# The same instructions in another order: an RWKV-7 and gMLP layer whose engine queues are filled by a scheduler that asks a different model of the machine

## The chip, the cores and the metric

The program runs on one core of one Trainium2 chip. A core has five engines with a queue each: TensorE (PE, with its weight loads shown apart as PEld), VectorE (DVE), ScalarE (ACT), GpSimd (POOL) and SyncE (SP). Each works through its queue strictly in the order in which the program was built, and waits on semaphores for the others and for DMA transfers. The metric is the device time of one execution in microseconds. Less is better.

## The reference, cut to what matters

One layer (DEPTH is 1) of a decoder trunk with 1024 channels, for 512 prompt tokens and 8 x 4 sample tokens, 544 columns in all:

```python
proj = xn @ w_in                      # [r | k | v | u | v_g | gate_A | gate_B]
rkv = rkv + (rkv_prev - rkv) * mu_rkv # token shift
decay = exp(-exp(w_log)); a = sigmoid(a0 + (xa @ a1) @ a2); g = sigmoid(xg @ g1) @ g2
def step(S, inp):                     # 16 heads of 64, one token after the other
    sa = einsum('bhij,bhj->bhi', S, -kk_t)
    S = S * w_t + sa * (kk_t * a_t) + v_t * k_t
    return S, einsum('bhij,bhj->bhi', S, r_t)
y = head_norm(y) + sum(rf * kf * r_k) * vf ; o_a = y * g
o_b = gelu(u) * chunk_mix(layernorm(gelu(v_g)))
mixed = sigmoid(ga) * o_a + sigmoid(gb) * o_b ; h = h + rmsnorm(mixed @ w_out)
h = h + rmsnorm(relu(rmsnorm(h) @ w_up)**2 @ w_down)
h = h + sigmoid(h @ w_pg) * (p @ w_pe)
```

Results and inputs are float32.

## The kernel before, in words

**Dense products.** Channels lie on the partitions, tokens on the free axis, in two halves of 288 and 256 columns. A weight block is fetched by SP (L201), rounded to a short form `w_hi` by ScalarE (L191), and the remainder `w_lo` is formed by VectorE (L192). `dense` (L209, its matmul is L214) then issues three matmuls for each 128 rows of weights: `w_hi` by `xh`, `w_hi` by `xl`, `w_lo` by `xh`. Most of TensorE's instructions are these; the text calls them dense matmuls. They do not depend on the recurrence, so they are what TensorE can do while the recurrence waits.

**Time mixing** goes by 8 pairs of heads, and its steps for a pair p are generators:

- `front(p)` (L395) makes r, k, v, the decay and the products of keys inside chunks (matmul L486, VectorE's mask L488 writes `M`), and stores part of `M` to DRAM through POOL's queue (`scr`, L504).
- `solve(p)` (L606) inverts small triangular blocks: POOL fetches them (`Xi`, L612), 28 short VectorE instructions in sequence (L619 and L621) invert them, POOL stores and fetches again (`solved`, L623, then `XD`, L627), VectorE transposes (`XN`, L632), and four rounds of small matmuls (L637, L645, L658, L667) finish the matrix `TT` that the chain needs.
- `chain(p)` (L677) carries the state over 8 chunks. Each chunk is a loop of matmul L687, ScalarE copy L691, matmul L701, ScalarE and VectorE L702 and L703, matmul L706, VectorE L717 (which writes `ZV` for the next chunk's L687). L689 and L707 add to the output and hang beside the loop.
- `samples(p)` (L552) does the sample tokens (L567, L593, L601 among others).
- `back(p)` (L727) normalises the output per head: sums over heads (L349, L350), rows to ScalarE (L358), POOL spreads them over partitions (`st`, L361), VectorE takes an inverse square root (L267 to L274, L364, L365), POOL brings it back (`invy`, L369), TensorE spreads it (L377), and elementwise steps (L740 to L752) with the gate's matmuls L748 to L751 follow.
- `gates(q)` (L755) holds 96 dense matmuls a pair and the elementwise steps L773 to L779; `mixed_in` (L786) turns the result into the operand `hh` or `mx` of the product with w_out (L792, L793).

**What sets the order.** `weave` (L813) interleaves the generators by planned shares (`SPAN`, `GATES`) and so gives each instruction its place in program order; that place is its priority. The Tile framework then keeps, for each engine, a list of instructions whose operands it thinks ready, by a model of how long everything takes, and emits the one of highest priority among them. Every engine's queue is thus fixed when the program is built. The product with w_out, the feed-forward product up, down and the last gate follow after the 8 pairs; they are dense matmuls with their weights streamed. The call that opens the framework's context is L1370 in `kernel`.

## Time and profile before

| | |
|---|---|
| time, median of two runs | 1194.06 us (1193.26 and 1194.86) |
| profiled execution, its own time | 1195.11 us |
| span of the profile | 1193.3 us |
| TensorE busy, weight loads busy | 1159.7 us (97%), 1086.1 us (91%) |
| VectorE, ScalarE, GpSimd busy | 815.6 us (68%), 579.7 us (49%), 108.0 us (9%) |
| granted TensorE clock, mean | 0.999 |
| first chunk of the chain of pair 0, last L706 of pair 7 | 220.5 us, 658.05 us |

The time of the profiled execution lies 1.8 us above its span. Busy time of TensorE is from modelled ends of pipelined matmuls, which overlap each other in the rows: the distance from start to start is what a matmul takes of the queue, not the duration in its row. An `x2` behind a row of the trace says that two instructions are merged in it.

### The profile page before, as it was taken

The numbers are of one execution on the slowest core, as the hardware profiler recorded it, in microseconds if no ns is written. First come the engines' busy times: TensorE is split into PE (matmuls) and PEld (weight loads), VectorE is DVE, ScalarE is ACT, GpSimd is POOL, SyncE is SP. The second block draws the span as 40 slices with busy tenths as digits, with TensorE's granted clock in tenths as the row PEclk, the third lists the DMA queues.
The fourth block names the chain that finished last, engine by engine and source line by source line (L and its number), as shares of the span: only waits on it lengthen the run. The fifth ranks groups of instructions, "written<-read, shape, count | busy, mean of one in ns | idle before, by whom it ended". The sixth has DMA issues, their size and how long they took to land.

```text
span 1193.3 us, 26307 instructions
## 1 busy us (share of the span) xinstructions
PE 1159.7 (97%) x10262; PEld 1086.1 (91%) x10262; DVE 815.6 (68%) x2251; ACT 579.7 (49%) x1406; POOL 108.0 (9%) x199
## 2 busy tenths in 40 slices
PE   7999998999899999999999999999999999999998
PEld 7999997888788888888878998999999999999998
DVE  6795778687878888887876646844563464465584
ACT  6646336557474747464655546642232232233352
POOL 0000012202230221122110000000000000000000
PEclk9999999999999999999999999999999999999999
DMA  6243253211222123141331452222222222222322
GB/s 203 72 126 114 100 159 114 86 50 46 63 74 83 48 64 99 34 118 44 112 95 55 131 171 72 91 81 89 88 89 89 89 89 89 89 89 89 116 73 83
DMA packets 68236, 109.33 MB, mean 92 GB/s; under 512 B 13712, under 2 KB 19760, under 8 KB 68112
## 3 DMA queue, kind: packets, MB, share of 16 engines
q1 hardware_dynamic: 60224, 103.94, 27.6%
q0 software_dynamic: 7600, 3.50, 1.8%
q8 instruction: 81, 1.33, 0.5%
q14 instruction: 43, 0.35, 0.1%
q10 hardware_dynamic: 288, 0.21, 0.1%
HBM read 94.40 MB, written 13.00 MB: 90 GB/s over the span
## 4 chain that ended last, share of the span: by engine, by line
PE 72%; DVE 12%; DMA 7%; ACT 6%; issue 2%; SPq 1%; POOL 0%; DVEq 0%; ACTq 0%; POOLq 0%
PE ps_d L214 47%; PE ps_s L214 3%; PE ps_s L486 2%; PE ps_b L214 2%; PE ps_m L214 2%; DVE w_lo L192 2%; ACT w_hi L191 2%; PE ps_cx L687 1%; PE ps_cx L701 1%; PE ps_cx L706 1%; DMA w_raw<-in_wout 1%; DMA w_raw<-in_wpg 1%; PE ps_cy L707 1%; DVE KR L456 1%; PE ps_m L601 1%
## 5 line engine op out<-in xcount | busy, mean ns | idle before, releaser
L192 DVE TENSOR_TENSOR w_lo<-w_raw,w_hi 128x512 fp32r<-128x512 f32 (+1 forms) x288 | 195.5, 681 | 174.0 <-ACT w_hi L191 169.9
L191 ACT CAST w_hi<-w_raw 128x512 fp32r<-128x512 f32 (+1 forms) x288 | 176.2, 613 | 275.9 <-PE ps_d L214 190.1
L214 PE MATMUL ps_d<-xh,w_hi 128*128 128x256 f32 (+3 forms) x832 | 249.4, 300 | 3.5 <-ACT w_hi L191 2.5
L214 PE MATMUL ps_d<-xl,w_hi 128*128 128x256 f32 (+3 forms) x832 | 246.9, 297 | 0.0
L214 PE MATMUL ps_d<-xh,w_lo 128*128 128x256 f32 (+3 forms) x832 | 246.9, 297 | 0.0
L214 PE MATMUL ps_d<-hh,w_hi 128*128 128x288 f32 (+1 forms) x1200 | 227.7, 288 | 0.0
L214 PEld LDWEIGHTS ps_d<-hh,w_hi 128*128 128x128 f32 x1200 | 188.8, 188 | 0.0
L214 PE MATMUL ps_d<-hh,w_lo 128*128 128x288 f32 (+1 forms) x600 | 173.6, 289 | 0.0
L214 PEld LDWEIGHTS ps_d<-xh,w_hi 128*128 128x128 f32 x832 | 157.5, 189 | 7.5 <-ACT w_hi L191 2.9
L214 PEld LDWEIGHTS ps_d<-xl,w_hi 128*128 128x128 f32 x832 | 157.6, 189 | 4.0 <-issue 3.2
L214 PEld LDWEIGHTS ps_d<-xh,w_lo 128*128 128x128 f32 x832 | 157.1, 189 | 2.2 <-issue 0.8
L214 PE MATMUL ps_d<-ax,w_hi 128*128 128x288 f32 (+1 forms) x704 | 133.3, 288 | 0.0
L214 PEld LDWEIGHTS ps_d<-hh,w_lo 128*128 128x128 f32 x600 | 112.8, 188 | 0.2 <-DVE w_lo L192 0.2
L214 PEld LDWEIGHTS ps_d<-ax,w_hi 128*128 128x128 f32 x704 | 110.3, 188 | 0.4 <-issue 0.2
L214 PE MATMUL ps_d<-ax,w_lo 128*128 128x288 f32 (+1 forms) x352 | 101.5, 288 | 0.0
L214 PEld LDWEIGHTS ps_d<-ax,w_lo 128*128 128x128 f32 x352 | 66.2, 188 | 0.0
L1256 ACT ACTIVATE ax<-t 128x288 fp32r<-128x288 f32 (+1 forms) x64 | 27.5, 430 | 45.4 <-DVE t L1255 45.2
L214 PE MATMUL ps_d<-gx,w_hi 128*128 128x288 f32 (+1 forms) x192 | 41.4, 309 | 6.8 <-ACT gx L853 6.0
L697 ACT ACTIVATE ZP<-ZV,Fp 64x64 f32<-64x64 f32 x96 | 33.1, 345 | 20.7 <-DVE ZV L717 17.3
L214 PEld LDWEIGHTS ps_d<-gx,w_hi 128*128 128x128 f32 x192 | 32.3, 199 | 8.1 <-ACT gx L853 6.0
L1257 DVE TENSOR_TENSOR t<-t 128x288 f32<-128x288 f32 (+1 forms) x64 | 28.1, 439 | 15.7 <-ACT ax L1256 15.3
L361 POOL DMA_DIRECT2D st<-rows x32 | 16.2, 511 | 243.9 <-ACT rows L358 176.8
(455 smaller groups left out, 2295.4 us busy)
## 6 DMA issues: line engine op xcount, KB each, us to landing
w_raw<-in_win SPq DMA_DIRECT2D x112, 256.0 KB, 2.8
w_raw<-in_wup SPq DMA_DIRECT2D x64, 256.0 KB, 2.7
w_raw<-in_wdn SPq DMA_DIRECT2D x64, 256.0 KB, 2.8
w_raw<-in_wout SPq DMA_DIRECT2D x16, 256.0 KB, 3.1
w_raw<-in_wpg SPq DMA_DIRECT2D x16, 256.0 KB, 2.9
w_raw<-in_lora SPq DMA_DIRECT2D x10, 256.0 KB, 2.8
xt<-in_xt SPq DMA_DIRECT2D x8, 276.0 KB, 5.4
ud<-u SPq DMA_DIRECT2D x8, 272.0 KB, 2.2
```

The costliest lines, as they stand in the source:

```text
L191: act.copy(out=hi, in_=raw)
L192: dve.tensor_tensor(out=lo, in0=raw, in1=hi, op=ALU.subtract)
L214: pe.matmul(out, lhsT=w[wi][k - k0], rhs=x[xi][k][:, cols[0]:cols[1]], start=start and n == 0 and j == 0, stop=stop and n == len(ks) - 1 a ...
L361: gp.dma_start(out=st[32 * h:32 * h + 32], in_=rows[h:h + 1].rearrange("o (a b) -> o a b", b=17))
L456: dve.tensor_tensor(out=KR[r, :, 0, h], in0=c3(kk)[r], in1=E[r, :, 0:64], op=ALU.mult)
L486: pe.matmul(p_[:, 256 * ci:256 * ci + 256], lhsT=BK[:, c + ci].rearrange("p a t -> p (a t)"), rhs=KR[:, c + ci].rearrange("p a h t -> p (a ...
L601: pe.matmul(p_[r], lhsT=s["BKTs"][r], rhs=SX[r], start=True, stop=True)
L687: pe.matmul(px[:, 0:128], lhsT=flat(M[:, c, 0]), rhs=flat(ZV[:, c]), start=True, stop=True)
L697: act.activation(out=ZP[r], in_=zv[h][r], func=AF.Copy, scale=F[r, c + 1, 0:1])
L701: pe.matmul(px[:, 0:128], lhsT=TT[:, c], rhs=Xc, start=True, stop=True)
L1256: act.activation(out=hi, in_=t, func=AF.Square)
L1257: dve.tensor_tensor(out=t, in0=t, in1=t, op=ALU.mult)
```

## The change

One argument is added where the framework's context is opened:

```diff
-    with tile.TileContext(nc) as tc:
+    with tile.TileContext(nc, schedule_with_timeline_sim=True) as tc:
         _program(tc, a, o)
```

With it the scheduler's readiness times come from its other model of the machine. The priorities are the same, and so are the instructions, except that ScalarE gets two more activation table loads (at L437 and L1004), because functions from different tables now alternate once more. The order on every engine differs. Three places are shown. Names carry a number, which tells instances of a tile apart.

TensorE, from the L687 of chunk 1 of the chain of pair 6 (`ps_cx_8774`, `ZV_7445`). `SV`, `SX` and `BKTs` belong to the samples, `xh` and `xl` to dense matmuls of `gates`. Before:

```order
L687 MATMUL ps_cx_8774<-ZV_7445,M_7226 128x128
L689 MATMUL ps_cy_8581<-KR_1632,ZV_7445 128x128
L593 MATMUL ps_m_8856<-Ms_7248,SV_7446 64x32 x2
L214 MATMUL ps_d_8951<-xh_93,w_hi_8888 128x256
L701 MATMUL ps_cx_8782<-Xc_8777,TT_2132 128x128
L214 MATMUL ps_d_8951<-xl_101,w_hi_8888 128x256
L214 MATMUL ps_d_8951<-xh_93,w_lo_8889 128x256
L601 MATMUL ps_m_8946<-SX_8947,BKTs_7271 64x512
L706 MATMUL ps_cx_8786<-ZV_7445,BKT_7258 128x128
L707 MATMUL ps_cy_8581<-M_7226,ZV_7445 128x128
```

With the change:

```order
L687 MATMUL ps_cx_8774<-ZV_7445,M_7226 128x128
L689 MATMUL ps_cy_8581<-KR_1632,ZV_7445 128x128
L701 MATMUL ps_cx_8782<-Xc_8777,TT_2132 128x128
L706 MATMUL ps_cx_8786<-ZV_7445,BKT_7258 128x128
L707 MATMUL ps_cy_8581<-M_7226,ZV_7445 128x128
L687 MATMUL ps_cx_8791<-ZV_7445,M_7226 128x128
```

The dense and sample matmuls that stood between the steps of the chain stand earlier now. From the L687 of chunk 1 to that of chunk 7 of this pair there are 87 dense matmuls before and none after; for pair 7 there are 70 and 15.

TensorE, behind the head sums (L349, L350 with `selw`) of the last pair, whose normalisation ends time mixing. `mx` and `hh` are operands of the product with w_out, `invy` is the head inverse that these sums lead to. Before, with 113 dense matmuls between the L350 and the first L377:

```order
L349 MATMUL ps_b_9554<-hs_hi_9550,selw_85 2x256
L350 MATMUL ps_b_9554<-hs_lo_9551,selw_85 2x256
L214 MATMUL ps_d_9696<-xl_107,w_hi_9639 128x256
...
L214 MATMUL ps_d_9962<-mx_9733,w_lo_9971 128x288
L377 MATMUL ps_b_9722<-invy_118,selt_83 128x288
L214 MATMUL ps_d_9963<-mx_9730,w_hi_9970 128x256 x2
```

With the change, with 29 between them:

```order
L349 MATMUL ps_b_9554<-hs_hi_9550,selw_85 2x256
L350 MATMUL ps_b_9554<-hs_lo_9551,selw_85 2x256
L214 MATMUL ps_s_9966<-hh_9908,w_lo_10133 128x288
...
L214 MATMUL ps_m_9967<-hh_9920,w_lo_10133 128x256
L377 MATMUL ps_b_9722<-invy_118,selt_83 128x288
L377 MATMUL ps_b_9724<-invy_118,selt_83 128x256
L748 MATMUL ps_b_9757<-GH0_114,l2hi_9752 128x288
```

What moved out from behind L350 are the dense matmuls of the last gates and most of the product with w_out; they stand ahead of it now.

POOL, the end of its queue: the solve of pair 7 (`Xi_8638`, `solved1_154`, `XD_8941`) and the head inverses of the pairs 5, 6 and 7 (`st` and `invy`). Before:

```order
L504 DMA scr_8238<-M_8211 32x8x32 x4
L612 DMA Xi_8638<-scr_8238 32x16x16 x2
L361 DMA st_8556<-rows_8539 32x1x17 x2
L369 DMA invy_118<-q_8574 1x32x17 x4
L623 DMA solved1_154<-Xi_8638 32x16x16 x2
L627 DMA XD_8941<-solved1_154 32x8x32 x4
L361 DMA st_9138<-rows_9121 32x1x17 x2
```

With the change:

```order
L504 DMA scr_8238<-M_8211 32x8x32 x4
L612 DMA Xi_8638<-scr_8238 32x16x16 x2
L361 DMA st_8556<-rows_8539 32x1x17 x2
L623 DMA solved1_154<-Xi_8638 32x16x16 x2
L369 DMA invy_118<-q_8574 1x32x17 x4
L627 DMA XD_8941<-solved1_154 32x8x32 x4
L361 DMA st_9138<-rows_9121 32x1x17 x2
```

The store of the solved blocks stands ahead of the head inverse of pair 5 now, behind it before. In the feed-forward half TensorE's instructions move by 24 places at most.

## Rows read from the trace of the kernel before

**Rows 1.** The page: span, and engines' busy time, share and instructions.

```profile
span 1193.3 us, 26307 instructions
PE 1159.7 (97%) x10262; PEld 1086.1 (91%) x10262; DVE 815.6 (68%) x2251; ACT 579.7 (49%) x1406; POOL 108.0 (9%) x199
```

**Rows 2.** Stretches: length; busy PE, PEld, DVE, ACT, POOL; clock, DMA share, GB/s.

```profile
200.00:570.00 370.00, 357.80 (x3701) 311.18 (x3699) 303.01 (x1002) 217.03 (x611) 76.53 (x138) 1.00 0.24 67
760.00:1193.00 433.00, 428.19 (x3409) 426.57 (x3407) 234.94 (x506) 143.71 (x292) 0.00 (x0) 1.00 0.29 90
```

**Rows 3.** Chain of waits, 20 to 26 us: start, duration, what.

```profile
22.11 1.59 PE ps_b L214 x12
23.71 1.41 PE ps_cx L214 x12
```

**Rows 4.** PE's timeline, 250 to 255 us, the chain's rows: start, duration, what.

```profile
250.97 0.46 PE L687 MATMUL ps_cx<-ZV,M 128*128 128x128 f32 x2
...
251.79 0.49 PE L701 MATMUL ps_cx<-Xc,TT 128*128 128x128 f32 x2
...
252.84 0.49 PE L706 MATMUL ps_cx<-ZV,BKT 128*128 128x128 f32 x2
...
254.11 0.46 PE L687 MATMUL ps_cx<-ZV,M 128*128 128x128 f32 x2
```

**Rows 5.** Chain of waits, 603 to 624 us: start, duration, what.

```profile
605.30 0.22 PE ps_cy L707 x2
605.52 1.00 PE ps_m L601 x2
```

**Rows 6.** PE's timeline, 568 to 691 us.

```profile
568.68 1.46 PE L486 MATMUL ps_s<-KR,BK 128*128 128x256 f32 x6
...
620.77 0.70 PE L637 MATMUL ps_m<-XN,M 16*32 16x32 f32 x60
...
658.05 0.42 PE L706 MATMUL ps_cx<-ZV,BKT 128*128 128x128 f32 x2
...
665.55 0.28 PE L350 MATMUL ps_b<-hs_lo,selw 128*2 128x256 f32 x1
...
679.93 0.29 PE L377 MATMUL ps_b<-invy,selt 128*128 128x288 f32 x1
...
690.26 0.42 PE L214 MATMUL ps_d<-hh,w_hi 128*128 128x288 f32 x2
```

**Rows 7.** POOL's timeline, 570 to 680 us, DMA issues: start, duration, what [idle before].

```profile
577.54 1.44 POOL L612 DMA_DIRECT2D Xi<-scr  x2 [3.74 <-DMA scr<-M]
...
603.51 1.35 POOL L623 DMA_DIRECT2D solved<-Xi  x2
607.26 2.31 POOL L627 DMA_DIRECT2D XD<-solved  x4 [2.41 <-PE ps_d L214]
...
673.59 1.96 POOL L369 DMA_DIRECT2D invy<-q  x4 [5.75 <-PE ps_d L214]
```

**Rows 8.** VectorE's timeline, 582 to 687 us.

```profile
582.97 0.17 DVE L619 TENSOR_TENSOR tmpi<-Xi 64x14 f32<-64x14 f32 x1 [1.48 <-DMA Xi<-scr]
...
602.04 0.18 DVE L621 TENSOR_TENSOR Xi<-Xi,tmpi 64x14 f32<-64x14 f32 x1
...
620.03 0.44 DVE L632 STREAM_TRANSPOSE XN<-XD 128x256 f32<-128x256 f32 x1
...
683.42 0.72 DVE L742 TENSOR_TENSOR Y<-Y,sv 128x544 f32<-128x544 f32 x1 [0.91 <-ACT Y L741]
...
686.91 0.41 DVE L752 TENSOR_TENSOR Y<-Y,ps_b 128x256 f32<-128x256 f32 x1
```

**Rows 9.** DMA issues, 664 to 680 us: count, KB each, us to landing.

```profile
invy<-q POOLq DMA_DIRECT2D x4, 2.1 KB, 1.6
```

**Rows 10.** A stretch, columns as in the second group.

```profile
623.00:628.00 5.00, 4.52 (x60) 3.81 (x60) 1.43 (x6) 2.95 (x8) 0.00 (x0) 0.66 0.37 111
```

**Rows 11.** Groups by line, ScalarE: count | busy us, mean ns | idle before.

```profile
L1004 ACT ACT_TABLE_LOAD x4 | 5.1, 1283 | 0.1
```

## The prediction, written before the changed kernel ran

> **What bounds the kernel now.** I read the page first: TensorE is busy for 1159.7 of 1193.3 us, no other engine for more than 68% [rows 1]. Whatever the change does, it does by adding to or taking from the time that TensorE's queue spends waiting. Then the stretches: in the feed-forward half weight loads are busy for 426.57 of 433.00 us, so matmuls stand back to back; in the middle, where the pairs run, for 311.18 of 370.00 us [rows 2]. All that can be won or lost lies in time mixing. Third, prices. Twelve dense matmuls of 288 columns take 1.59 us and twelve of 256 columns 1.41 us in the chain of waits, 133 and 118 ns each [rows 3]; a chain or float32 matmul of 128 columns takes 0.22 us, a sample matmul L601 0.50 us [rows 5]. With these I priced the stretches of TensorE's queue between two landmarks in either order ("row cost" below): a stretch cannot be shorter than its row cost, nor than the path of waits through the other engines between the same landmarks. Where the row cost was above the path, the recurrence was hidden; where it falls below, the difference is lost.
>
> **The paths.** One chunk of the chain takes 0.82 us from L687 to L701, 1.05 on to L706 and 1.27 on to the next L687, 3.14 us where nothing else is late [rows 4]. The solve of pair 7 begins behind the last mask matmul L486, which starts at about 569.8 us (the last of six in 1.46 us), and ends at L637, 620.77 us [rows 6]. On it lie: 7.7 us until `Xi` is issued at 577.54 [rows 7], 5.4 until the first of the 28 inversion steps at 582.97, 19.2 until the last ends at 602.22 [rows 8], 3.9 until `XD` is issued [rows 7] with the store's 1.35 and its landing, 4.7 for the issue and as long a landing again (2.4), and 0.7 from `XN` at 620.03 to L637 [rows 8, 6]. The head inverse goes from L350 at 665.55 [rows 6] to the end of the last `invy` issue, 675.55 [rows 7], and the landing of 1.6 us [rows 9]: 11.6 us.
>
> **The change, part by part.** The instructions are the same but for two table loads, and only their order is in question. I walked the two orders of TensorE, POOL and VectorE from landmark to landmark.
>
> *A, the solve of pair 7.* From the last L486 to L637 there are 165 dense matmuls and 44.5 us of row cost before, against 51.0 us real: 6.5 us lost. With the change there are 21 dense matmuls and 17.6 us. The path then rules. The 28 steps last 0.20 us from one to the next (0.40 from L619 to L619) [rows 8], 5.7 us if VectorE does nothing else between, and 12.4 us if it does all of the 16 others that its new order puts there. So the path is 28 to 35 us; I take 33, near the upper end because a queue is strict and the others stand in it. Lost: 33 - 17.6 = 15.4 us, **+8.9** on before (bounds +4 to +11). That POOL now stores the solved blocks ahead of the head inverse of pair 5 saves up to the 1.96 us of four `invy` issues [rows 7], if that inverse would otherwise be ready first; it moves them in front of `XD` instead, so I give it nothing.
>
> *B, the chain of pair 7.* From L637 to the last L706: real 37.3 us [rows 6], row cost 30.8 us before (101 dense matmuls), 6.5 lost. Now 63 dense matmuls, 26.5 us. Of these only 15 stand between the L687 of chunk 1 and that of chunk 7, with 13.8 us of row cost against 6 x 3.14 + 1.87 = 20.7 us of path up to the last L706: 6.9 us lost. The rounds L645 to L667 lie closer too; I add 4 us for them and for small losses, less than the 6.5 of before. **+4.4** (0 to +9). The chain of pair 6, with no dense matmul between its steps, costs nothing of its own, since it runs while the solve of A is waited for; if A were short, it would be 10 us.
>
> *C, the end of time mixing.* From the last L706 to the first product on the last `hh`: real 32.2 us [rows 6], row cost 30.7 before (230 dense matmuls): 1.5 lost. Inside, 113 dense matmuls, 14.2 us, cover the head inverse of 11.6 us. Now 29 of them, 3.6 us, stand there: 8.0 lost. From L377 to the last `hh` matmul it is 10.3 us before [rows 6], of which 2.8 pass between the end of L742 (684.14) and the second L752 (686.91) in waiting for matmuls that stood late [rows 8]; the path is about 7.6. Row cost there falls from 9.9 to 4.0 us: 3.6 lost. **+10.1** (+7 to +12).
>
> The dense matmuls missing in A to C are done earlier, among pairs 0 to 5, at the same price each. Where did TensorE need them there? Its chains have groups of about 24 between steps (3.0 us), close to the whole 3.14 us of a chunk, where before there was 0.5 to 1 us at each step. By row cost against the path their latency loses 10.5 us now and 9.1 before, and the samples of pair 1 stand with gaps of 0.2 to 0.4 us. **+2** for all of it (-8 to +8).
>
> *The clock.* TensorE's granted clock is full except once: 0.66 over 623 to 628 us [rows 10], right behind the small matmuls of the solve, with dense matmuls around. That is one part at 1.2 GHz, the rest at 2.4. The cost is 5 x 0.34 = 1.7 us. After A and C TensorE will have stood idle more than there; two such stretches cost 3.4. **+3** (0 to +8). The Trainium skill says, on the page "TensorE: Matmul & The Clock Gate", section "HAM oscillation — how this bites in real kernels", that a kernel whose matmul bursts are shorter than the waits between them is set back to the low clock at each; by that rule the bursts of A and C would be slow throughout, which is the third rival. The one drop in the trace fits it, and no wait of such length is there to test it.
>
> *The rest.* Two more table loads on ScalarE take 1.28 us each [rows 11]; it is busy 49% [rows 1], and copies of the chain wait behind them at worst: 0 (to +2.6). The same skill's page "ScalarE: Activation LUTs", section "What ACT_TABLE_LOAD costs", adds a drain and gives 2.66 us a load, 5.3 us for both at worst; the rows show 0.1 us of idle before the loads and do not show a drain. In the feed-forward half the order moves by 24 matmuls at most, under 3.2 us of queue; SP's fetches keep their order, so 0.
>
> Sum: 8.9 + 4.4 + 10.1 + 2 + 3 = 28.4 us. The profiled execution took 1195.1 us, 1.0 above the median of the runs, so 1195.1 + 28.4 - 1.0 = 1222.5; I write **1222**.
>
> **Rivals.** *First, not slower:* the large dense groups win time in pairs 0 to 5. In 200 to 570 us weight loads are idle for 58.8 us of 370, where the feed-forward rate would leave 5.6 [rows 2]: about 53 us, 9 for each pair, lost in waits at the steps. If groups of 24 halve that, by letting ScalarE and VectorE answer while TensorE has 3 us to do, 27 us come back and the time is 1222 - 27 = 1195. It decides from 0.8 us a pair on: then the 4.5 us between 1222 and the bound of "slower" are gone. For it speaks that 3.0 us cover each single step of 0.8 to 1.3 us; against it that a group longer than the step delays the chain, and that by the path formula the pairs lose 1.4 us more. Chance 0.2. *Second, nothing changes:* waits only change places, because the row costs by which A to C lose are made up where the shifted matmuls no longer wait; 1195 +- 8. That asks for 28 us of other losses to vanish by chance: 0.05. *Third, the clock:* in A and C and in the chains of pairs 6 and 7 TensorE runs at 1.2 GHz. The 2.8 and 3.6 us of dense matmuls there cost double, the 4.0 too, and some 42 links grow by 0.2 us, the 0.22 us of a chain matmul [rows 5] once more: 10 + 8 = 18 us, 1240. One drop behind small matmuls speaks for it; the full clock in sample stretches against. 0.13. *Fourth, solves of the earlier pairs:* row costs from L486 to L637 of pairs 2 to 6 are 33 to 37 us now, 45 to 62 before, and the path is 28 to 42 us (with the 19.2 us of inversion steps as seen). If they lose 3 us each, 15 us more: 1237. Chance 0.12.
>
> **How the numbers follow.** The forecast has 0.5, with its own range of 1210 to 1236 (half-widths of A 3.5, B 4.5, C 2.5, the early part 8 and the clock 4 added as squares, and a little more). The range of 1199 to 1244 takes it in whole, most of the third and fourth rival, and half of the first. About 2%, 24 us, can be told from no change in this kernel: under 1170 is faster, above 1218 slower. Slower: two thirds of the forecast and nearly all of the third and fourth, 0.33 + 0.24, with a little more for a shape I did not see: 0.60. Same: the rest of the forecast, the first and second, 0.36. Faster needs 52 us from pairs 0 to 5, all that is lost there: 0.04.
>
> **What will show it.** Right: from 570 us on, TensorE is idle for about 15 us between the last L486 and L637, then 1 us in each chunk of the chain of pair 7, 8 us ahead of the last L377 and 3 to 4 behind it; feed-forward as long as before; pairs 0 to 5 within 8 us. Wrong: weight loads clearly denser between 200 and 570 us (first rival), a clock of 0.5 for more than 7 us in all (third), gaps of over 2 us ahead of L637 in pairs 2 to 6 (fourth). If no gap stands ahead of the last L377, the price of dense matmuls was not the measure of that cover.

## The result, and the profile after

The changed kernel takes **1307.13 us** (two runs, 1301.90 and 1312.36) against 1194.06: a ratio of 1.095, with a 95% interval of 1.076 to 1.114. The forecast was 1222 us, within 1199 to 1244. The direction was right, the size was not: 113 us instead of 28. The profiled execution is the longer of the two runs, 1312.36 us, with a span of 1310.6.

The page of the changed kernel: span, TensorE's busy time, and its busy share and granted clock in 40 slices, in tenths.

```profile
span 1310.6 us, 26366 instructions
PE 1212.9 (93%) x10262; PEld 1137.6 (87%) x10262; DVE 823.2 (63%) x2251; ACT 581.8 (44%) x1408; POOL 108.2 (8%) x199
PE   7999999989999898988997887899999999999988
PEclk9899999987988796988997877999999999999999
```

The span is 117.3 us longer than in [rows 1]. TensorE's rows are busy for 53.2 us more with the same instructions, and the time in which it is not busy rises from 33.6 to 97.7 us, 64.1 more. The first part comes with the clock: its mean is 0.934 where it was 0.999, so some 173 us of the span (2 x 0.066 x 1310.6) ran at 1.2 GHz, where it was about 3 (2 x 0.34 x 5 in [rows 10]). The slices with a low digit all lie ahead of the feed-forward half.

Where in the program? The stretches between four landmarks (first L486 of pair 0, last L486 of pair 7, last chain matmul L706, and the product with w_out), columns as in [rows 2]; first before, then after.

```profile
0.00:143.00 143.00, 135.96 (x1019) 130.62 (x1020) 104.28 (x267) 85.35 (x174) 4.94 (x13) 1.00 0.39 124
143.00:570.00 427.00, 411.51 (x4095) 361.88 (x4095) 348.30 (x1126) 244.49 (x669) 86.92 (x156) 1.00 0.27 77
570.00:658.00 88.00, 85.60 (x985) 71.58 (x985) 63.37 (x203) 49.53 (x143) 13.21 (x24) 0.98 0.30 89
658.00:690.00 32.00, 31.01 (x241) 29.93 (x240) 21.89 (x49) 16.12 (x33) 2.96 (x6) 1.00 0.51 149
```

```profile
0.00:163.00 163.00, 145.81 (x1083) 140.79 (x1084) 109.20 (x280) 91.92 (x182) 4.92 (x13) 0.98 0.36 116
163.00:687.00 524.00, 483.49 (x4628) 434.82 (x4627) 371.48 (x1162) 261.83 (x705) 87.07 (x156) 0.90 0.26 74
687.00:775.00 88.00, 71.41 (x553) 55.84 (x552) 47.81 (x165) 38.87 (x116) 13.29 (x24) 0.75 0.15 41
775.00:810.00 35.00, 26.02 (x164) 23.80 (x164) 15.99 (x40) 12.48 (x27) 2.96 (x6) 0.80 0.40 128
```

The last L486 of pair 7 stands at 687 instead of 570 us: all 117 us of delay are there already. From there to the end it takes 623.6 us after and 623.5 before. But the third and fourth stretch hold 432 and 77 rows of matmuls fewer: matmuls of some 46 us of row cost (26.9 in A, 4.3 in B, 14.6 in C, by the counts and prices of the prediction; three quarters of it are dense matmuls) have moved ahead of the landmark. So the end of time mixing lost 46 us more than before, and what lies ahead of it lost 117 - 46 = 71 us more. For the first the prediction had 23.4, for the second 2.

What such a loss looks like: three stretches around the end of pair 3, columns as above, and TensorE's timeline in the middle one.

```profile
478.00:495.00 17.00, 15.54 (x184) 15.26 (x183) 14.34 (x60) 11.39 (x32) 9.63 (x18) 1.00 0.32 86
495.00:519.00 24.00, 19.75 (x214) 16.11 (x213) 15.77 (x42) 9.98 (x28) 0.00 (x0) 0.50 0.06 18
519.00:546.00 27.00, 25.46 (x177) 21.47 (x178) 16.77 (x52) 11.56 (x33) 3.64 (x6) 1.00 0.34 97
```

```profile
499.50 0.76 PE L687 MATMUL ps_cx<-ZV,M 128*128 128x128 f32 x2
500.06 0.63 PE L689 MATMUL ps_cy<-KR,ZV 128*128 128x128 f32 x2
500.62 1.06 PE L658 MATMUL ps_m<-XN,M 32*32 32x32 f32 x32
501.62 0.61 PE L748 MATMUL ps_b<-GH,l2hi 128*128 128x288 f32 x1
...
502.75 0.63 PE L701 MATMUL ps_cx<-Xc,TT 128*128 128x128 f32 x2
503.03 0.80 PE L377 MATMUL ps_s<-invk,selt 128*128 128x288 f32 x2
503.76 1.06 PE L667 MATMUL ps_m<-TT,M 32*32 32x32 f32 x32
507.77 0.58 PE L748 MATMUL ps_b<-GH,l2hi 128*128 128x256 f32 x1 [2.95 <-DVE Y L752]
...
508.79 0.63 PE L706 MATMUL ps_cx<-ZV,BKT 128*128 128x128 f32 x2
509.21 0.63 PE L707 MATMUL ps_cy<-M,ZV 128*128 128x128 f32 x2
```

From 494.5 to 519.4 us there is no dense matmul. Two things are to be seen. L701 to L706 takes 6.0 us where [rows 4] has 1.05: L706 stands behind an L748 of another pair, and that one waits for VectorE, which is 2.95 of the 6.0 us. And the clock is 0.50 throughout: from L706 to L707 it is 0.42 us, where [rows 5] has 0.22 for such a matmul. The stretches on either side, with dense matmuls, ran at 1.00.

### The profile page after: what moved, and what is told of

Its sections match the earlier page's. It is cut to its first block, busy times and chain, and to the rows that moved or that the text cites. A ratio compares the mean times of both kernels' runs of the same rounds, so it can differ in the third digit from the quotient of the medians.

```text
span 1310.6 us, 26366 instructions
## 1 busy us (share of the span) xinstructions
PE 1212.9 (93%) x10262; PEld 1137.6 (87%) x10262; DVE 823.2 (63%) x2251; ACT 581.8 (44%) x1408; POOL 108.2 (8%) x199
## 5 line engine op out<-in xcount | busy, mean ns | idle before, releaser
L191 ACT CAST w_hi<-w_raw 128x512 fp32r<-128x512 f32 (+1 forms) x288 | 176.2, 614 | 263.0 <-PE ps_d L214 167.2
L214 PE MATMUL ps_d<-hh,w_hi 128*128 128x288 f32 (+1 forms) x1200 | 231.6, 290 | 2.9 <-DVE hh L1323 1.2
L214 PEld LDWEIGHTS ps_d<-xh,w_hi 128*128 128x128 f32 x832 | 160.2, 193 | 12.4 <-ACT u L1004 2.1
L214 PEld LDWEIGHTS ps_d<-xl,w_hi 128*128 128x128 f32 x832 | 160.8, 193 | 1.3
L214 PEld LDWEIGHTS ps_d<-xh,w_lo 128*128 128x128 f32 x832 | 160.2, 193 | 1.3 <-issue 0.2
L687 PE MATMUL ps_cx<-ZV,M 128*128 128x128 f32 x128 | 32.5, 341 | 16.4 <-DVE ZV L717 13.4
L486 PE MATMUL ps_s<-KR,BK 128*128 128x256 f32 x128 | 42.9, 482 | 4.1 <-DVE BK L462 4.1
L706 PE MATMUL ps_cx<-ZV,BKT 128*128 128x128 f32 x128 | 33.3, 348 | 12.4 <-DVE ZV L703 12.2
```

The source lines that it names most:

```text
L191: act.copy(out=hi, in_=raw)
L214: pe.matmul(out, lhsT=w[wi][k - k0], rhs=x[xi][k][:, cols[0]:cols[1]], start=start and n == 0 and j == 0, stop=stop and n == len(ks) - 1 a ...
L486: pe.matmul(p_[:, 256 * ci:256 * ci + 256], lhsT=BK[:, c + ci].rearrange("p a t -> p (a t)"), rhs=KR[:, c + ci].rearrange("p a h t -> p (a ...
L687: pe.matmul(px[:, 0:128], lhsT=flat(M[:, c, 0]), rhs=flat(ZV[:, c]), start=True, stop=True)
L706: pe.matmul(pz[:, 0:128], lhsT=s["BKT"][:, c], rhs=flat(ZV[:, c]), start=True, stop=True)
```

## The experiments

In all of them the instructions are those of the kernel, and only the queues differ, unless the text says so. "Held" orders are built by edges that fix the place in an engine's queue and add no wait; the wanted order is taken from a build of either kernel. An engine that is left free is scheduled anew around the held ones. The code is shown shortened.

**Which engine's order?** First TensorE's queue alone as changed, then TensorE's alone as before.

```diff
     with tile.TileContext(nc, schedule_with_timeline_sim=False) as tc:
         _program(tc, a, o)
+        q = _scout(arrays, True)[PE]            # TensorE's queue of the changed kernel
+        for x, y in zip(q, q[1:]): _behind(tc, ins[y], x)
```

> The scheduler of before, but TensorE's queue is forced into the order that the changed kernel has; the four other engines are scheduled around it by the model of before. Theory A (TensorE's order is the cause: the dense matmuls run ahead of the chain, so that the last third of each pair's chain links stands bare): 1270 to 1320 us, with 120 us or more at 1.2 GHz. Theory B (the order on VectorE, ScalarE, POOL and SP is the cause, by steps of the recurrence that stand behind other work there): under 1225 us.

Measured 1330.39 us (ratio 1.111, 1.100 to 1.123), mean clock 0.936, 171 us at 1.2 GHz. Theory A's side, 10 us above its range.

```diff
-    schedule_with_timeline_sim=False ... q = _scout(arrays, True)[PE]
+    schedule_with_timeline_sim=True  ... q = _scout(arrays, False)[PE]
```

> The scheduler of the change, but TensorE's queue is forced into the order that it has before; the other engines are scheduled around it by the changed model. Theory A: 1190 to 1220 us and at most 10 us at 1.2 GHz. Theory B: over 1270 us.

Measured 1306.60 us (1.091, 1.081 to 1.102), mean clock 0.968. Theory B's figure, so neither theory stands alone. Nor do the two runs set TensorE's order against that of the others, because the free engines follow the held one. Counted in the queues as built, VectorE's instructions stand 22.8 places on average from where they stood before in the former run and 2.5 from where they stand in the changed kernel; in this run it is 4.4 and 23.0. For ScalarE it is 16.2 and 0.9, then 1.3 and 16.1. So the former run is nearly the changed kernel on every engine, and TensorE's new order among the others' old ones was not run. This run is nearly the kernel before, with small moves on the other engines, and those alone cost some 110 us. TensorE's longest waits in this run, and then what the kernel before has for the same lines:

```profile
PE ps_s L486 <- DVE BK L462: 13.2, 5, 4.8
PE ps_cx L706 <- DVE ZV L703: 10.1, 12, 1.6
PE ps_cx L701 <- ACT Xc L691: 7.2, 13, 1.6
PE ps_cx L687 <- DVE ZV L717: 6.0, 10, 1.6
```

```profile
PE ps_s L486 <- DVE BK L471: 3.2, 3, 2.7
PE ps_cx L706 <- DVE ZV L703: 1.8, 5, 0.5
PE ps_cx L687 <- DVE ZV L717: 1.3, 6, 0.2
```

The figures are us in total, how often, and the longest. Before, L486's wait for L462 and L701's for L691 are not among TensorE's nineteen longest; L471 also writes `BK`. The matmuls are where they were; what they wait for comes later from VectorE and ScalarE.

**How much does each add?** The old order is held on one engine after the other.

```diff
-    for e in (PE,):
+    for e in (PE, DVE):            # then (PE, DVE, Activation)
```

> The changed scheduler with the queues of TensorE and VectorE forced into the order of before; ScalarE, POOL and SP are scheduled around them by the changed model. With TensorE's queue alone it was 1307 us. If VectorE's order holds what was left of the cost: 1195 to 1230 us. If it lies with ScalarE or the two engines that issue the transfers: 1270 us or more.

Measured 1244.08 us (1.042, 1.036 to 1.049).

> As the former with ScalarE's queue forced too, so that only POOL and SP are left to the changed model. If the three compute engines hold all of the cost: 1192 to 1215 us. If the order in which POOL and SP issue transfers costs much by itself: 1240 us or more.

Measured 1200.75 us (1.0056, 1.0029 to 1.0084). So with TensorE's order as before, holding VectorE's as well wins 63 us, then ScalarE's 43, and POOL and SP are left with 8. These are steps in this sequence; in another the shares could differ. ScalarE surprised me: in the run with TensorE and VectorE held (1244 us), nine in ten of its instructions, casts and others alike, stand within two places of where they stood, and these moves cost 43 us.

**What moved on them?** A weight cast waits until TensorE gives a weight buffer back: on the page of the kernel before, ScalarE is idle for 275.9 us ahead of its 288 casts (L191), 190.1 of them until a dense matmul ended. So casts alone were held.

```diff
+    for e in (DVE, Activation):    # e10: PE and DVE held whole, this for Activation alone
+        for n in before[e]:
+            if n in cast: _behind(tc, ins[n], last)
+            else: last = n
```

> The changed scheduler with TensorE's queue in the order of before (1307 us so far), and with each weight cast (w_hi on ScalarE, w_lo on VectorE) held behind the other instruction that it follows on its engine before; all else is free. Theory D (the model lets casts pass steps of the recurrence; a cast then waits for TensorE to give a weight buffer back, and what stands behind it waits too): 1215 to 1250 us. Theory E (it is the order of the other rows among themselves): 1285 us or more.

Measured 1288.11 us (1.079, 1.066 to 1.091): 18 of some 110 us came back by the medians, and the intervals of the two runs overlap. Theory E's figure.

> As the run with the queues of TensorE and VectorE in the order of before (1244 us), with the casts on ScalarE held as in the former. Theory D: 1200 to 1218 us, since ScalarE's whole queue forced gave 1201. Theory E: 1235 us or more.

Measured 1226.39 us (1.027, 1.018 to 1.036): between the two, 18 of the 43 us.

> All five queues forced into the order of before, but on ScalarE the instructions other than weight casts stand in the order that the changed model gives them around TensorE and VectorE of before; the casts keep their places (each with as many others ahead of it as before). Theory D: 1192 to 1206 us. Theory E: 1225 to 1245 us.

Measured 1221.89 us (1.023, 1.013 to 1.034), 29 us above the kernel before. Theory D explains under half of ScalarE's part; the rest comes from the other rows. They may be copies of the solve or of the products of keys that now stand ahead of a copy of the chain; no run singles them out. In this run TensorE waits 6.7 us for the copy L691 at L701, and 9 of the 22 us by which the chain ends later are lost ahead of the first chunk. Moving the casts alone was not tried.

**Dense matmuls and chain links.** The chain links are the 192 matmuls L687, L701 and L706 of the eight chains. Of the 191 gaps between them 22 hold no dense matmul before, and 99 after. By pairs 0 to 7 these bare gaps are 3, 3, 2, 2, 4, 4, 1, 3 before and 10, 12, 12, 12, 9, 2, 21, 21 after; in the pairs 0, 2, 3 and 4 seven to nine of them follow one another towards the end. So dense matmuls were held back: none further ahead of the links than before.

```diff
+    for n in before[PE]:
+        if n in link: last = n
+        elif n in dense and last and link[last] >= 0:   # e4: >= 6, e12: <= 5 (pair)
+            _behind(tc, ins[n], last)
```

> The changed kernel with one constraint: no dense matmul may stand further ahead of the 192 chain links than it does before; all the rest is left to the changed scheduler. Theory A in its narrow form (it is the dense matmuls alone that ran ahead): 1195 to 1230 us. If the small matmuls' order or the other engines matter as much: 1250 us or more.

Measured 1293.37 us (1.080, 1.070 to 1.091), mean clock 0.963. The narrow form of theory A fails: with the cover back in place (20 bare gaps in the queue as built), the rest of the new order costs some 100 us.

> The same constraint for the links of the pairs 6 and 7 alone, that is for the end of time mixing, where the prediction had put its sum of 23 us. By the changed kernel's trace the end (675 to 825 us) loses some 45 us more than before and the pairs 0 to 5 and what lies ahead of them some 60: theory A gives 1255 to 1280 us. If the loss of the end is what the prediction said: about 1285. If what is won at the end is lost again because the dense matmuls that move back leave the earlier pairs no fuller: within 10 us of the changed kernel, 1300.

Measured 1302.05 us (1.088, 1.077 to 1.098), 5 us below the changed kernel and not to be told from it. The last L706 comes 26 us earlier (748.9 against 775.2), and the rest then takes 17 us longer, because 164 dense matmuls that were moved back stand there. In the queue as built, pair 5 now has 18 bare gaps where the changed kernel has 2: the bareness has moved to another pair.

> The changed scheduler, with dense matmuls held back to where they stand before among the chain links of the pairs 0 to 5 alone; the links of the pairs 6 and 7 stand as bare as the change leaves them (one group of 131 and then mostly none). Against the run that holds them everywhere (1293 us) only the end of time mixing differs, for which the prediction summed 8.9 + 4.4 + 10.1 = 23 us. If that sum is right: 1310 to 1325 us. If the end costs what its stretch in the changed kernel's trace lost on top of before, 45 us: 1330 to 1345. If what the end lacks is covered by something else: 1285 to 1300.

Measured 1291.28 us (1.083, 1.081 to 1.085): 2 us below the run that holds them everywhere. The queue as built is not what I had expected of it: the dense matmuls held back from the pairs 0 to 5 stand ahead of pair 6 and in it, which has 8 bare gaps instead of 21, and 197 of them stand between the last L486 and L637 of pair 7, where the run that holds them everywhere has 129 and the changed kernel 21. As bare as in the changed kernel are the chain of pair 7 (21 gaps) and what follows the last L706. From the last L486 to the last L706 it takes 106.1 us against 87.5, 18.6 more; 6.1 of these are won ahead of that stretch and 14.9 behind it. So the bareness of the prediction's B and C costs nothing here, in a kernel in which the others' orders cost some 100 us already. That of A was not run by itself.

**The clock.** In the changed kernel, all five queues held, four unused matmuls were set behind each of the 101 links with fewer than two dense matmuls behind them: of 256 columns, then of 8.

```diff
+    if (p, c, stage) in _BARE:
+        for _ in range(4):
+            pe.matmul(px[:, 256:256 + 2 * w] ..., lhsT=blk, rhs=blk[:, 0:w] twice)   # w = 128; e6: w = 4
```

> The changed kernel with all five queues in exactly its order, and four more matmuls (128x128 weights, 256 columns, result unused) behind each of the 101 chain links that have fewer than two dense matmuls behind them: 404 matmuls, 48 us of row cost at 118 ns. Theory C (the granted clock: TensorE's rows are busy for 53 us more than before, because 174 us run at 1.2 GHz, and the bare links are where it falls): under 90 us at 1.2 GHz, and 1245 to 1290 us in spite of the added work. If the low clock is only a by-product of waiting for other engines, which set the time: 1305 to 1350 us, since part of the 48 us comes on top.

Measured 1315.76 us (1.102, 1.093 to 1.112). The clock did what theory C says (mean 0.973, 71 us at 1.2 GHz instead of 173). The time did not fall; it lies in the range of the other side.

> The control of the former: the same 404 matmuls at the same places, but of 8 columns in place of 256. Theory C: 1.2 GHz for 150 us or more as in the changed kernel, 1300 to 1325 us. If it is the mere presence of instructions there that helps: as the former.

Measured 1357.23 us (1.137, 1.130 to 1.145), mean clock 0.913, 235 us at 1.2 GHz, above both sides' figures. I had expected narrow matmuls to be short. They are not. TensorE's groups of the added matmuls (count, busy us, mean ns), wide and then narrow, and each kernel's stretch from 480 to 545 us:

```profile
L1412 PE MATMUL ps_cx<-blk 128*128 128x256 f32 x404 | 76.1, 312 | 0.0
480.00:545.00 65.00, 57.59 (x576) 50.49 (x576) 45.46 (x145) 30.64 (x86) 9.57 (x18) 0.92 0.21 64
```

```profile
L1412 PE MATMUL ps_cx<-blk 128*128 128x8 f32 x404 | 83.4, 312 | 0.0
480.00:545.00 65.00, 60.03 (x565) 54.87 (x563) 41.84 (x139) 28.43 (x77) 12.12 (x22) 0.76 0.13 35
```

From start to start they take 120 and 112 ns at the full clock, 214 and 213 at 1.2 GHz (medians of the distances between neighbours). Each of them loads its own weights, and the starts of these loads lie as far apart (118 and 112 ns at the full clock, 214 and 213 at 1.2 GHz), so this is the distance of a load and its matmul together. The two kernels are thus alike but for the clock and some 3 us (404 x 8 ns), and 164 us more at 1.2 GHz cost 41.5 us, 0.25 us for each. By this price the 173 us of the changed kernel cost 43 of its 113 us. That is an estimate, since the price comes from kernels with 404 matmuls more; as the bound from above I take the 53 us of TensorE's additional busy time. In the former run the added matmuls took 66 us of the queue. That they hid a gain from the better clock would fit, and is not shown.

**The model or the fit?** The program's shares (SPAN) may have been fitted to the old model's order, so that any other would cost.

```diff
-    "chain": (0, 0.55), "solve": (0.05, 1.2)
+    "chain": (0, 0.62), "solve": (0.05, 1.1)
-    "samples": (0.1, 0.8), "gates": (0, 1)              # second shift
+    "samples": (0.15, 0.85), "gates": (0.05, 1.05)
```

> The kernel before with two shares of the interleaving shifted a little (chain ends at 0.62 instead of 0.55 of a round, solve at 1.1 instead of 1.2), under the model of before. Theory G (the changed model orders badly whatever the program order): 1193 to 1208 us. Theory H (the program order was fitted to the old model, and any other order costs): 1215 to 1270 us.

Measured 1197.80 us (1.003, 0.999 to 1.007).

> The same shifted shares under the changed model. Theory G: 1295 to 1320 us, about 100 above the former. Theory H: 1270 to 1320 us, 20 to 70 above the former.

Measured 1317.17 us (1.101, 1.087 to 1.115).

> Another shift under the model of before: gates from 0.05 to 1.05 instead of 0 to 1, samples 0.15 to 0.85 instead of 0.1 to 0.8. Theory G: 1193 to 1208 us. Theory H: 1215 to 1270 us.

Measured 1206.18 us (1.008, 1.005 to 1.012).

> The second shift under the changed model. Theory G: 1295 to 1320 us. Theory H: 1270 to 1320 us, 20 to 70 above the run with the same shares under the old model.

Measured 1313.48 us (1.098, 1.085 to 1.111). Theory G: with either shift the old model keeps its time within 1% and the changed one stays 107 to 119 us above it. So the cost is not a fit of these shares that such a shift would lose.

## Why the prediction was wrong

*What bounds the kernel:* right in part. TensorE's queue is the bound and the change lies in time mixing: from 810 us to the end the changed kernel takes 500.6 us, and the kernel before takes 503.3 from 690, although the matmuls of the last gate move by up to 120 places and not 24. But TensorE does not only wait more: beside the 64 us in which it is not busy there are 53 us of longer rows.

*A, the solve:* the path was nearly right: 37.0 us from the last L486 (687.0) to L637 where I took 33, with 17.6 us of row cost. So 19.4 us are lost instead of 15.4, +12.9 on before instead of +8.9. Only 7.5 us of the 37.0 are idle time, where I had put 15; the granted clock was 0.77. *C, the end,* came out within 2 us as a whole. TensorE's timeline of the changed kernel, then one row of the kernel before:

```profile
686.37 1.03 PE L486 MATMUL ps_s<-KR,BK 128*128 128x256 f32 x4
...
724.04 0.60 PE L637 MATMUL ps_m<-XN,M 16*32 16x32 f32 x46 [0.21 <-DVE XN L632]
...
775.06 0.38 PE L706 MATMUL ps_cx<-ZV,BKT 128*128 128x128 f32 x2
...
785.10 0.28 PE L350 MATMUL ps_b<-hs_lo,selw 128*2 128x256 f32 x1
...
795.10 0.58 PE L377 MATMUL ps_b<-invy,selt 128*128 128x288 f32 x1 [6.02 <-DMA invy<-q]
...
801.25 0.85 PE L214 MATMUL ps_b<-mx,w_hi 128*128 128x288 f32 x2 [0.51 <-DVE Y L752]
...
806.04 0.41 PE L214 MATMUL ps_d<-hh,w_hi 128*128 128x288 f32 x2
```

```profile
691.45 0.43 PE L214 MATMUL ps_d<-hh,w_hi 128*128 128x288 f32 x2
```

L350 to L377 is 10.0 us (11.6 forecast), of which 6.0 are the wait for the inverse (8.0 forecast). L377 to the first product on the last `hh` (806.04) is 10.9 us where I had 7.6: the last 4.8 of them are 21 dense matmuls, most of them at the low clock. From the last L706 it is 31.0 us against 16.1 of row cost, 14.9 lost. Before it was 2.7 and not 1.5, since the row at 690.26 that I took is a product on an earlier `hh`, and the one on the last starts at 691.45. That makes +12.2 where I had +10.1, with one error against the other, so some of it is luck. *B, the chain of pair 7,* was short by more than half: from L637 to the last L706 it is 51.0 us against 26.5 of row cost, 24.5 lost where I had 10.9, so +18.0 instead of +4.4. Its clock was low for about half of it (0.73 from 724 to 775 us), which I had priced once, elsewhere.

Two readings behind these sums were off, each by about 1 us. The dense matmuls counted from the L687 of chunk 1 "to that of chunk 7" are counted to the last L706; in pair 7 all 15 stand between its last L701 and last L706, and six chunks are wholly bare. And in [rows 5] the two merged instructions are one L601, which takes 1.00 us and not 0.50.

*The step that failed* is "+2 for all of it (-8 to +8)", the pairs 0 to 5 and what lies ahead of them, which measured 71 us. I had read that their links have "groups of about 24" dense matmuls, and taken the groups that I saw for all of them. The count by links shows what the mean hid: 57 bare gaps in the pairs 0 to 5 where there were 18. In the pairs 0, 2, 3 and 4 a pair's dense matmuls are used up in its first links, and towards its end it is as bare as the end that I had priced; pair 1 begins with seven bare gaps, and pair 5 has two in all. But bare links do not make the 71 us by themselves: with the dense matmuls of these pairs held where they stood the kernel took 1291 us, 16 less than 1307.

*The second failed step* is that only TensorE's order was priced, and of the others' order three places. With TensorE's queue as before, the others' orders cost some 110 us by themselves. VectorE, busy for 68%, had a price in one place, and ScalarE, busy for 49%, for its table loads alone; but in a queue that is worked off in order a wait holds up everything behind it. The two failed steps and the clock overlap, and how they share the 113 us of the changed kernel is not shown.

*The clock,* +3 us, cost some 43 by the price above. The third rival had the mechanism and a chance of 0.13, but a price of 18. The Trainium skill ("TensorE: Matmul & The Clock Gate", section "HAM oscillation — how this bites in real kernels") has the rule that a kernel whose matmul bursts are shorter than the waits between them is set back to the low clock at each, and counts half of the time at the low clock as lost. The trace agrees only in part: at the end of pair 3 the clock was 0.50 from 495 to 519 us, where the rows are busy for 19.75 of 24 us and no wait is longer than 2.95 us, and the price here was 0.25 us and not 0.5. Nor does the one drop before fit this rule, though the prediction says that it does: in the 15 us ahead of it TensorE waits for 0.48 us at most.

*That A to C add up to a part of the kernel's loss* is not shown: their stretches lost 43 us more, but the three runs with held dense matmuls took 1293, 1302 and 1291 us, whether the end was covered, as in the first two, or bare in B and C. Dense matmuls are a fixed stock; what covers one wait is missing at another.

*The first rival,* large groups that win time in the early pairs, did not happen: in 163 to 687 us weight loads are busy for 83%, in 143 to 570 us before for 85%. *The fourth,* later solves, did not show its sign: ahead of the first L637 of a pair TensorE is idle for 1.9 us in pair 3 and for at most 0.2 us in the others.

**What stays open.** Why the changed model sets 17 to 24 dense matmuls, 2.1 to 3.0 us, between links that take 0.82 to 1.27 us [rows 4]: that it takes links for longer or dense matmuls for shorter than they are would fit, and was not tried. Nor was it found which of the inversions on ScalarE cost the 29 us, or what TensorE's new order costs with the others' orders of before. No version beat the kernel before.

## What to carry to other kernels

Where an order changes, count the cover at every link of the recurrence and look at the distribution, before adding up the places that look worst: a stock of independent work that is spent early in a round leaves its end bare, here in four of the first six pairs. Price the order of every engine that stands in a strict queue between two steps of the recurrence, however idle it is on average; five queues are one schedule, and moves of a few places on the other engines cost as much here, around TensorE's old order, as the whole change. And give a bare stretch of small matmuls two prices, the wait and the clock: here 0.25 us for each us at 1.2 GHz.

## What the runs showed of the hardware that was not expected

A matmul with 128x128 weights of its own and 8 columns of this type takes nearly as long from start to start as one with 256 columns, 112 against 120 ns; at 1.2 GHz it is 213 against 214. And with the same instructions in another order the time at 1.2 GHz rose from about 3 us to 173; in the one stretch shown TensorE's rows are busy for 82% (19.75 of 24 us).
